# A transformer layer in split fp32: a new order at the front (opening of the row tiles, first convolution block among the query tiles, taps dealt from there)

## The chip, the core and the metric

The kernel runs on one core of a Trainium2 chip. TensorE multiplies matrices into PSUM, VectorE, ScalarE and GpSimd work on elements, and SyncE (SP) issues most transfers between HBM and SBUF. The metric is the device time of one execution in microseconds. The kernel before takes 1634.73 us (median of three runs, 1633.79 to 1635.66).

## The reference

One layer over 1024 rows of width 1024, all in float32. The parts that the change touches are the normalised rows, the memory branch's queries and the convolution; the rest stands as one line each.

```python
xn = rms_norm(x, norm_mix)
proj = xn @ w_in          # NSA queries, keys, values, gates; conv_in; q_mem; g_merge

# branch A: br_nsa, sparse attention (compressed, selected and windowed keys), 8 heads

# branch B: convolution
a, ag = jnp.split(conv_in, 2, axis=-1)
u = a * jax.nn.sigmoid(ag)
u = causal_depthwise_conv(u, conv_w, width=31) + conv_b
u = jax.nn.silu(layer_norm(u, conv_ln_g, conv_ln_b))
br_conv = u @ w_conv_out

# branch C: attention into 256 memory rows
qm = rms_norm(q_mem.reshape(b, s, 4, 128), mem_qk_norm[0])
kvm = rms_norm(mem, norm_mem) @ w_mem_kv
# ... softmax(qm km) vm, then br_mem = o_m @ w_mem_out

gm = jax.nn.sigmoid(g_merge).reshape(b, s, 3, 1024)
h = x + (gm[:, :, 0] * br_nsa + gm[:, :, 1] * br_conv + gm[:, :, 2] * br_mem) @ w_out
hn = rms_norm(h, norm_ffn)
return h + (silu(hn @ w_gate) * (hn @ w_up)) @ w_down
```

## The kernel before

**Arithmetic.** Every operand of a large product is split into a high part (a cast to `fp32r`, L131) and a low part (the value less its high part, L132). One product of the reference is three products on TensorE (high by high, low by high, high by low), gathered in one PSUM bank; `mm` (L146) emits them and lists them in `products`. A *unit* is a piece of a weight matrix of 128 partitions by 1024 elements with both its parts: ScalarE makes the high part, VectorE or GpSimd the low part.

**Rows.** The 1024 rows of x are eight row tiles of 128 rows, taken in four pairs. `norm_row` squares a row tile on ScalarE, takes the root there, and scales the tile on VectorE (L218). `turn_pair` then turns a pair by 16 TensorE transposes of 128x128 (L238) into four banks; ScalarE writes the high parts with the gain (L228, listed in `his`) and VectorE the low parts (L230, listed in `los`), eight instructions each. The rows so turned are `XN`, the operand of every projection.

**Memory queries.** `queries(ws, t, 0, rqm)` projects row tile t on the 512 query columns: 24 products of 128x512 (`wide_proj`, four weight units), then a copy on ScalarE (L345), a store to HBM by SP (L348), the square on ScalarE (L349) and its sum by heads on VectorE (L350). The loop runs over all eight tiles, and the second, third and fourth pair are turned behind tiles 1, 2 and 4. `square_queries` fetches the stored queries later and normalises and turns them (`t<-qraw`, `qt_m<-t`).

**Convolution.** Behind the queries come 35 small rows (31 taps of the filter, bias, two layer norm vectors: L444 to L448), which four transposes turn into `cw` (L451). Then four convolution blocks of 128 channels: two units, and for each half of the rows 24 products for the sigmoid's operand (`pg`), the sigmoid on ScalarE, 24 products for `pa`, and their product into `U`. Two `square_queries` follow each block. `weight_sums` (in the first block) loads pieces of `w_out`, makes differences of them on VectorE (`sub`, L128) and stores them as `tw`.

**Taps.** The filter itself is 124 VectorE instructions (31 for each of 4 blocks, `tap`, L485 and L486) of about 1000 columns. They are emitted at the end with a low priority and *dealt*: each is ordered behind a product of the list `products`, evenly by work, from `first_tap` (the count of products when the first convolution block is done) to the end of the projections. The turned keys (L745) come in the later part of that list.

**Filler.** The products of the merge gates (banks `pf`) have a low priority as well; TensorE takes them where nothing else is ready.

**What sets the order.** All instructions are emitted by one program in Python. A scheduler then orders each engine's queue by priority (mostly the order of emission) and by a model of the times; each engine runs its queue strictly in that order. `follow` and `add_manual_dep` add an order between two instructions without a wait on data. Banks, slabs and stages come from rotating pools.

Of the kernel before, what the change touches and what calls it, by code (L numbers as in the profile page):

```python
# [17 lines left out]
P = 128  # L18
# [21 lines left out]
def hybrid_layer_kernel(  # L40
# [127 lines left out]
    nc.vector.memset(ones, 1.0 / 512)  # L168
    strip = const([768], BF16, "strip")
# [40 lines left out]
    his, los = [], []  # L210
# [22 lines left out]
    def turned_pair(js, kp, after=None, at=None):  # L233
        b = bank([2, 256], at=at)
        for kk in range(2):
            k = 2 * kp + kk
            for tt in range(2):
                m = nc.tensor.transpose(b[:, kk, tt * P:(tt + 1) * P], js[tt][:, k * P:(k + 1) * P], ident)  # L238
                if after is not None:
                    follow(m, after, "tiles by turns with products")  # L240
        return b

# [5 lines left out]

    def rows2(src, r0):
        xs = slab([2, D], F32)  # L250
        for tt in range(2):
            nc.sync.dma_start(xs[:, tt, :], src[r0 + tt * P:r0 + (tt + 1) * P, :])
# [6 lines left out]
    def turn_x(tp):  # L259
        half, q = tp // 2, tp % 2  # L260
        if q == 0:
            for kp in range(4):
                XN[half][kp] = slab([2, 2, 512])
        turn_pair(xin[tp], 0, lambda kp: tuple(XN[half][kp][:, hl, :, q * 256:(q + 1) * 256] for hl in range(2)),
                  products[-12 if tp == 1 else -1][0] if tp else None)


    def unit(src, shape, alloc=wslab, eng=None, load=False, after=None):
# [8 lines left out]
        if after is not None:  # L277
            follow(m, after, "weights' cast behind attention's")
# [3 lines left out]
    def col_unit(w, c0, n=P, alloc=wslab, eng=None, load=False):  # L282
        return unit(w[:, c0:c0 + n].rearrange("(k p) c -> p k c", p=P), [w.shape[0] // P, n], alloc, eng,
                    load)
# [38 lines left out]

    def wide_proj(ws, t):

        o = bank([512])
        half, a = t // 4, (t % 4) * P
        if t == 0 and len(products) == 0:
            for k0 in (0, 4):
                for hx, hw in ((0, 0), (1, 0), (0, 1)):  # L330
                    for k in range(k0, k0 + 4):
                        mm(o, xn(hx, k, half, a, a + P), ws[k // 2][hw][:, k % 2, :], k + hx + hw == 0,
                           k == KT - 1 and hw == 1)
# [6 lines left out]
    def queries(ws, t, j, stat):  # L340
# [5 lines left out]
        if j == 0:  # L346
# [67 lines left out]
    ws = [wide_unit(w_in, C_QM, u, alloc=slab, eng=e) for u, e in enumerate((nc.vector, nc.gpsimd))]  # L414
    raw_w = [t4([2, 512]) for _ in range(2)]
    for u in range(2):
        nc.sync.dma_start(raw_w[u], wide_rows(w_in, C_QM, 2 + u))
    xin += [rows2(x, tp * 256) for tp in range(1, 4)]
    nc.sync.dma_start(gm, mem_qk_norm.to_broadcast([P, 2, P]))
# [4 lines left out]
    for raw, eng in zip(raw_w, (nc.gpsimd, nc.vector)):  # L424
        w_ = slab([2, 2, 512])
        m = nc.vector.tensor_copy(w_[:, 0], raw)
        follow(m, los[3], "behind the first tiles' parts")
        part = eng.tensor_tensor(w_[:, 1], raw, w_[:, 0].bitcast(F32), op=OP.subtract)
        if eng is nc.vector:
# [1242 lines left out]
```

## Time and profile before

| | us |
|---|---|
| median of three runs | 1634.73 |
| profiled execution | 1634.0 |
| its span (first to last instruction) | 1632.3 |
| TensorE busy | 1616.9 (99%) |
| TensorE's weight loads (beside its products) | 1361.7 (83%) |
| VectorE busy | 1097.7 (67%) |
| ScalarE busy | 759.1 (47%) |
| GpSimd busy | 662.3 (41%) |
| HBM read / written | 193.52 MB / 85.98 MB |

In the rows of the profile an engine is named PE (TensorE), PEld (TensorE's weight load), DVE (VectorE), ACT (ScalarE), POOL (GpSimd) or SP; a small q behind it is its sequencer. L345 is line 345 of the kernel. A row of the groups gives an operation, what it writes and reads, how often it runs, its busy time with the mean in ns, and the idle time of its engine ahead of it with what ended it. A row of the chain of waits gives when a step begins, how long it lasts, and in brackets how long it waited and for what. A row of the windows gives a stretch of time, its length, and then for each engine (PE, PEld, DVE, ACT, POOL) its busy time in that stretch with the number of its instructions, then the granted clock, the share of time in which the transfer engines were busy, and GB/s. A row of the transfers gives size and median time from issue to landing.

In the chain of waits, TensorE holds 92% of the span. The first products come at 10.8 us; before that lie loads, one row tile's scaling and its transposes.

### The profile page before, as it was taken

What the parts mean: (1) busy time and instruction counts of PE and PEld (TensorE: products, weight loads), DVE (VectorE), ACT (ScalarE), POOL (GpSimd) and SP (SyncE); (2) the same over time, 40 slices, a digit from 0 to 9 for tenths busy, and PEclk for the clock granted to TensorE, in tenths of its full rate; (3) what the DMA queues carried; (4) which work ended last, traced back from release to release, by engine and by line L of the source; (5) the groups of instructions that cost most, each with busy time, mean ns of one, the idle gap of its engine ahead of it and who ended that gap; (6) DMA issues with size and microseconds to landing.
All of it is one profiled execution on the core that took longest, in us unless ns stands there. A gap on an engine that the chain in (4) does not pass through costs nothing.

```text
span 1632.3 us, 22769 instructions
## 1 busy us (share of the span) xinstructions
PE 1616.9 (99%) x7952; PEld 1361.7 (83%) x7952; DVE 1097.7 (67%) x1821; ACT 759.1 (47%) x1404; POOL 662.3 (41%) x535
## 2 busy tenths in 40 slices
PE   8999999999999999999999999999999999999999
PEld 6887898888888888888888889888888888888887
DVE  6389989996676655654795968865455544476665
ACT  6211357634777756664684447332223222233332
POOL 2011003741777766654135341665556777300000
PEclk9999999999999999999999999999999999999999
DMA  8454457753555545546754453333234446893773
GB/s 293 170 170 118 134 163 202 240 166 109 154 172 174 172 138 152 164 143 231 241 179 157 165 194 136 97 113 114 90 112 147 142 152 199 314 383 101 238 232 117
DMA packets 254874, 281.03 MB, mean 172 GB/s; under 512 B 24404, under 2 KB 176260, under 8 KB 253222
## 3 DMA queue, kind: packets, MB, share of 16 engines
q1 hardware_dynamic: 247846, 266.98, 51.3%
q10 hardware_dynamic: 6912, 12.59, 2.1%
q8 instruction: 63, 1.03, 0.3%
q14 instruction: 53, 0.43, 0.1%
HBM read 193.52 MB, written 85.98 MB: 171 GB/s over the span
## 4 chain that ended last, share of the span: by engine, by line
PE 92%; DVE 3%; POOL 2%; issue 1%; DMA 1%; ACT 1%; SPq 0%; DVEq 0%; POOLq 0%; ACTq 0%
PE ps L146 52%; PE pf L146 19%; PE ps L1606 11%; PE ps L1374 4%; PE ps L1006 2%; PE pf L1606 1%; DVE slab L486 1%; PE ps L238 1%; PE pf L1374 1%; POOL slab L684 0%; PE ps L986 0%; DMA t<-qt_m 0%; DMA qt_n<-t 0%; POOL t L367 0%; DMA slab<-in_x_dram 0%
## 5 line engine op out<-in xcount | busy, mean ns | idle before, releaser
L146 PE MATMUL ps<-slab,wsl 128*128 128x512 f32 (+2 forms) x1688 | 362.5, 373 | 0.0
L146 PEld LDWEIGHTS ps<-slab,wsl 128*128 128x128 f32 x1688 | 298.3, 188 | 56.3 <-issue 1.0
L146 PE MATMUL pf<-slab,fsl 128*128 128x512 f32 x1260 | 320.9, 395 | 0.4 <-ACT fz L1081 0.4
L146 PEld LDWEIGHTS pf<-slab,fsl 128*128 128x128 f32 x1260 | 231.1, 188 | 44.0 <-ACT fz L1081 0.7
L486 DVE SCALAR_TENSOR_TENSOR slab<-slab,cw 128x1019 f32<-128x1019 f32 (+16 forms) x120 | 161.7, 1352 | 1.4
L1502 DVE TENSOR_TENSOR t<-ps,t 128x512 f32<-128x512 f32 x130 | 88.7, 687 | 105.8 <-PE ps L146 104.4
L146 PE MATMUL ps<-slab,fsl 128*128 128x512 f32 x660 | 155.9, 391 | 0.0
L146 PE MATMUL ps<-slab,slab 128*128 128x512 f32 (+1 forms) x628 | 150.9, 377 | 0.8 <-POOL slab L684 0.8
L146 PEld LDWEIGHTS ps<-slab,fsl 128*128 128x128 f32 x660 | 123.1, 188 | 25.5 <-issue 0.3
L146 PEld LDWEIGHTS ps<-slab,slab 128*128 128x128 f32 x628 | 112.5, 189 | 22.6 <-POOL slab L684 1.7
L1606 PE MATMUL ps<-wsl 128*128 128x512 f32 x495 | 118.9, 389 | 0.0
L1606 PEld LDWEIGHTS ps<-wsl 128*128 128x128 f32 x495 | 93.0, 188 | 19.2
L132 DVE TENSOR_TENSOR wsl<-st,wsl 128x1024 fp32r<-128x1024 f32 x58 | 82.6, 1428 | 29.3 <-ACT wsl L131 26.9
L146 PE MATMUL ps<-slab,qt 128*128 128x384 f32 (+6 forms) x400 | 95.6, 339 | 1.6 <-DVE sm L869 1.3
L131 ACT CAST wsl<-st 128x1024 fp32r<-128x1024 f32 x61 | 63.9, 1053 | 70.3 <-PE ps L146 25.0
L146 PE MATMUL ps<-wsl,slab 128*128 128x512 f32 (+1 forms) x480 | 95.3, 349 | 0.0
L131 ACT CAST wsl<-t 128x1024 fp32r<-128x1024 f32 x43 | 45.3, 1053 | 88.3 <-POOL t L128 35.4
L146 PE MATMUL ps<-t,slab 128*128 128x256 f32 (+1 forms) x404 | 86.2, 317 | 0.0
L132 POOL TENSOR_TENSOR slab<-slab,t 128x1024 fp32r<-128x1024 f32 (+1 forms) x28 | 63.0, 2250 | 55.8 <-ACT t L131 50.7
L146 PEld LDWEIGHTS ps<-wsl,slab 128*128 128x128 f32 x480 | 76.8, 189 | 10.4
L132 DVE TENSOR_TENSOR t<-ps,t 128x512 fp32r<-128x512 f32 (+2 forms) x96 | 61.0, 640 | 33.5 <-ACT t L131 32.7
L1515 POOL TENSOR_TENSOR t<-t,t 128x512 f32<-128x512 f32 x21 | 39.3, 1871 | 108.1 <-DVE t L1502 54.7
(270 smaller groups left out, 2950.9 us busy)
## 6 DMA issues: line engine op xcount, KB each, us to landing
t<-in_w_down_dram SPq DMA_DIRECT2D x70, 256.0 KB, 3.7
fst<-in_w_in_dram SPq DMA_DIRECT2D x24, 512.0 KB, 4.2
zd<-fz ACTq DMA_DIRECT2D x48, 256.0 KB, 2.0
slab<-wd SPq DMA_DIRECT2D x24, 512.0 KB, 4.0
t<-zd SPq DMA_DIRECT2D x24, 512.0 KB, 3.6
st<-in_w_gate_dram SPq DMA_DIRECT2D x22, 512.0 KB, 3.8
st<-in_w_up_dram SPq DMA_DIRECT2D x22, 512.0 KB, 4.1
ad<-t SPq DMA_DIRECT2D x44, 256.0 KB, 3.0
```

The source lines that it names most:

```text
L131: m = nc.scalar.copy(hi, src)
L132: return m, (eng or nc.vector).tensor_tensor(lo, src, hi.bitcast(F32), op=OP.subtract)
L146: m = nc.tensor.matmul(o, a, b, start=start, stop=stop)
L238: m = nc.tensor.transpose(b[:, kk, tt * P:(tt + 1) * P], js[tt][:, k * P:(k + 1) * P], ident)
L486: return nc.vector.scalar_tensor_tensor(acc[:, s:], u[:, :S - s], cw[:, ct, 30 - s:31 - s], acc[:, s:], op0=OP.mult, op1=OP.add)
L1006: nc.tensor.transpose(b[:, j - j0, h, :], tiles[h][:, j * P:(j + 1) * P], ident)
L1374: nc.tensor.matmul(B[j], a_(ha, k, j), w[:, hb, k % 2, :], start=start and k == 0 and n_ == 0, stop=stop and k == 3 and n_ == 2, skip_grou ...
L1502: nc.vector.tensor_tensor(o, a_, b_, op=OP.add)
L1515: nc.gpsimd.tensor_tensor(u4, u4, c22, op=OP.mult)
L1606: nc.tensor.matmul(B[t], a_, b_, start=start and k == 0 and j == 0, stop=k == FH - 1 and j == 2, skip_group_check=True)
```

## The change

It does six things, all within the program's first 100 us but for the taps.

1. **Constant products.** 26 bf16 products of a constant tile (`spin`, 128x256), whose result nobody reads, stand at the front of TensorE's queue.
2. **Opening.** `first_pair` turns the eight blocks of row tile 0 first, then those of row tile 1, into four banks. The four query units' raw values are all loaded ahead; the high parts of units 0 and 1 are made on VectorE, those of 2 and 3 on ScalarE behind the first pair's last high part; the low part of unit 2 on GpSimd, the others on VectorE, in a written order. Tiles 0 and 1 are multiplied by turns (`first_two`), and their last four products stand behind the second pair's transposes. Their copies stand behind that pair's high parts.
3. **Loads.** Three small loads (`gm`, `gn`, `w2s`) stand behind the row loads; the second pair's rows ahead of the gates' first weights, the third pair's rows behind them.
4. **First convolution block.** It runs behind the fourth query tile instead of the eighth, and the fourth pair of row tiles is turned inside it, between `pg` and `pa` of the first half. The small rows of the convolution and `weight_sums` move with it. Query tiles 4 to 7 follow.
5. **Taps.** `first_tap` is set behind that block, so that the 124 taps are dealt over a list that begins earlier.
6. **`square_queries`.** Three, three and two behind the blocks 1, 2 and 3, instead of two behind each of four.

The products of the layer are the same ones, in the same number.

```diff
+    spin = ones.bitcast(BF16)
+    b = psp[0].tile([P, 256], F32, tag="ps0", name=nm("ps"))
+    for _ in range(26):
+        nc.tensor.matmul(b, spin[:, :P], spin, start=True, stop=True)
...
     def turn_pair(src, g0, dests, after=None):
+        js = [src[:, tt, :] for tt in range(2)]
+        first = None if his else first_pair(js)
         for kp in range(4):
-            b = turned_pair([src[:, tt, :] for tt in range(2)], kp, after)
+            b = first[kp] if first else turned_pair(js, kp, after)
...
+    def first_pair(js):
+        banks, last = [bank([2, 256]) for _ in range(4)], None
+        for tt in range(2):
+            for k in range(KT):
+                m = nc.tensor.transpose(banks[k // 2][:, k % 2, tt * P:(tt + 1) * P], js[tt][:, k * P:(k + 1) * P], ident)
...
-        if t == 0 and len(products) == 0:
+        if not products:
+            first_two.append(bank([512]))
             for k0 in (0, 4):
-                for hx, hw in ((0, 0), (1, 0), (0, 1)):
+                for hx, hw, k1, k2 in ((0, 0, 0, 2), (1, 0, 0, 2), (0, 0, 2, 4), (1, 0, 2, 4), (0, 1, 0, 4)):
+                    for b, c in zip((o, first_two[0]), (0, P)):
...
-    ws = [wide_unit(w_in, C_QM, u, alloc=slab, eng=e) for u, e in enumerate((nc.vector, nc.gpsimd))]
-    raw_w = [t4([2, 512]) for _ in range(2)]
+    raw_w = [stage.tile([P, 2, 512], F32, tag="st", name=nm("st")) for _ in range(2)] + [t4([2, 512]) for _ in range(2)]
...
-    for raw, eng in zip(raw_w, (nc.gpsimd, nc.vector)):
+    for u in range(4):
         w_ = slab([2, 2, 512])
-        m = nc.vector.tensor_copy(w_[:, 0], raw)
-        follow(m, los[3], "behind the first tiles' parts")
+        high = (nc.vector.tensor_copy if u < 2 else nc.scalar.copy)(w_[:, 0], raw_w[u])
+        eng = nc.gpsimd if u == 2 else nc.vector
+        part = eng.tensor_tensor(w_[:, 1], raw_w[u], w_[:, 0].bitcast(F32), op=OP.subtract)
+        if u == 1:
+            tc.add_manual_dep(los[0], high.ins.name, ORDER, reason="low parts behind the first weights' high parts")
+        elif u > 1:
+            follow(high, his[7], "high part behind the first tiles'")
+        if u != 2:
+            follow(part, parts[-1] if u == 1 else los[7 if u else 3], "low part behind the first tiles'")
+    for m in los[4:8:2]:
+        tc.add_manual_dep(m, parts[1].name, ORDER, reason="low parts behind the first weights'")
...
-    for t in range(NT):
+    def memory_queries(t):
         queries(ws, t, 0, rqm)
-        if t in (1, 2, 4):
+        if t in (1, 2):
             turn_x((t + 2) // 2)
+            if t == 1:
+                tc.add_manual_dep(products[44][0], turns[-1].name, ORDER, reason="last products behind the second pair")
+                for m in copies:
+                    tc.add_manual_dep(m, his[-1].name, ORDER, reason="queries' copies behind the second pair")
+            rows_x(t // 2 + 2)
+    for t in range(4):
+        memory_queries(t)
...
-    for ct in range(4):
+    def conv_block(ct, between=None):
         for half in range(2):
             pg = chan_proj(wag, half)
+            if half == 0 and between is not None:
+                between()
...
+    conv_block(0, lambda: turn_x(3))
+    for t in range(4, NT):
+        memory_queries(t)
+    stat_rms(rqm)
+    for ct in range(1, 4):
+        conv_block(ct)
...
-        for t in (2 * ct, 2 * ct + 1):
+        for t in range(3 * ct - 3, min(3 * ct, NT)):
             square_queries(0, t, rqm)
```

How it stands in the engines' queues: a row is an instruction with its line, what it writes and reads (numbers tell buffers of one kind apart) and the semaphores that it waits for. First VectorE at the start, of before: `slab_142` holds the first pair of row tiles, `slab_153` unit 0, `st_151` its raw values, `slab_233` and `slab_236` units 2 and 3, `ps_...` turned blocks.

```order
L218 TENSOR_SCALAR slab_142<-slab_142,sm_190 128x1024 [waits DMAHW1_49,DVE_49]
L132 TENSOR_TENSOR slab_153<-st_151,slab_153 128x1024 [waits DMAHW4_49,Activation_49]
L230 SCALAR_TENSOR_TENSOR slab_193<-ps_197,gcol,slab_193 128x256 [waits PE_49,Activation_49]
...
L426 CAST slab_233<-t_10_161 128x1024 [waits DMAHW6_49]
L426 CAST slab_236<-t_11_162 128x1024 [waits DMAHW7_49]
L443 TENSOR_TENSOR spent<-spent 128x192 [waits DMAHW1_49]
L230 SCALAR_TENSOR_TENSOR slab_195<-ps_215,gcol,slab_195 128x256 [waits PE_49,Activation_49]
```

The same place of the change: `slab_254` and `slab_257` are units 0 and 1, `st_178` and `st_179` their raw values.

```order
L222 TENSOR_SCALAR slab_169<-slab_169,sm_211 128x1024 [waits DMAHW1_49,DVE_49]
L455 CAST slab_254<-st_178 128x1024 [waits DMAHW4_49]
L455 CAST slab_257<-st_179 128x1024 [waits DMAHW5_49]
L236 SCALAR_TENSOR_TENSOR slab_214<-ps_218,gcol,slab_214 128x256 [waits PE_49,Activation_49]
...
L457 TENSOR_TENSOR slab_254<-st_178,slab_254 128x1024 [waits DVE_49]
L457 TENSOR_TENSOR slab_257<-st_179,slab_257 128x1024 [waits DVE_49]
L236 SCALAR_TENSOR_TENSOR slab_216<-ps_220,gcol,slab_216 128x256 [waits PE_49,Activation_49]
```

The high parts of units 0 and 1 stand ahead of the tiles' low parts now, those of units 2 and 3 have left VectorE, and unit 1's low part stands behind unit 0's.

Second, SP's queue around the convolution's small rows, of the change (`t_82_516` holds the small rows, `t_80_508` is the copy of the fourth query tile, `t_91_546` to `t_94_549` are pieces of `w_out`). Before, it was the store of the eighth query tile that stood among these loads.

```order
L514 DMA t_94_549<-in_w_out_dram 128x2x512 [waits DMAHW0_49]
L520 DMA tw<-t_91_546 128x1024 [waits DMAHW1_49,DVE_49]
L487 DMA t_82_516<-in_conv_w_dram 31x512 [waits DMAHW2_49]
L376 DMA qraw<-t_80_508 128x512 [waits DMAHW3_49,Activation_49]
L488 DMA t_82_516<-in_conv_b_dram 1x512 [waits DMAHW4_49]
L489 DMA t_82_516<-in_conv_ln_g_dram 1x512 [waits DMAHW5_49]
L490 DMA t_82_516<-in_conv_ln_b_dram 1x512 [waits DMAHW6_49]
L496 DMA t_84_527<-in_cmp_pos_dram 16x2x128 [waits DMAHW7_49]
```

The three single rows and the position rows stand behind the store of the fourth query tile, which waits for ScalarE.

Third, TensorE's queue at the fourth pair of row tiles (`slab_171` before, `slab_192` in the change). Before:

```order
L146 MATMUL ps_487<-slab_236,slab_403 128x512 [waits DVE_49]
L238 MATMUL ps_518<-identr,slab_171 128x128 [waits DVE_49]
L238 MATMUL ps_527<-identr,slab_171 128x128 [waits PE_49]
...
L146 MATMUL ps_554<-slab_153,slab_400 128x512 x2
L238 MATMUL ps_518<-identr,slab_171 128x128 [waits DVE_49]
```

And in the change (`ps_578` is `pg` of the first half, `t_82_516` the convolution's small rows):

```order
L146 MATMUL ps_578<-slab_217,wsl_537 128x512 x6
L244 MATMUL ps_603<-identr,slab_192 128x128 [waits DVE_49,PE_49]
L244 MATMUL ps_630<-identr,slab_192 128x128 [waits Activation_49]
L493 MATMUL ps_521<-identr,t_82_516 128x34 [waits DMAHW5_49,DMAHW6_49,DMAHW4_49,DMAHW2_49]
L493 MATMUL ps_521<-identr,t_82_516 128x34 x3
L244 MATMUL ps_612<-identr,slab_192 128x128 [waits PE_49]
L244 MATMUL ps_603<-identr,slab_192 128x128 [waits DVE_49]
```

The four transposes of the small rows, with their wait for four loads, stand behind two of the fourth pair's blocks and ahead of the other fourteen; before, they stood among the products of the convolution.

More of the change, by code (lines that the diff above doesn't have):

```diff
@@ L240, in turned_pair @@
                     follow(m, after, "tiles by turns with products")
+        turns.append(m.ins)
         return b
+    def first_pair(js):
[3 more added lines that the diff above has]
+                m = nc.tensor.transpose(banks[k // 2][:, k % 2, tt * P:(tt + 1) * P], js[tt][:, k * P:(k + 1) * P], ident)
+                if last is not None:
+                    follow(m, last, "first row's blocks in front")
+                last = m.ins
+        return banks
     XN = [[None] * 4 for _ in range(2)]
@@ L247, in xn @@
         return XN[half][k // 2][:, hl, k % 2, a:b]
+    row_loads = []
     def rows2(src, r0):
@@ L277, in unit, with col_unit @@
         if after is not None:
-            follow(m, after, "weights' cast behind attention's")
+            follow(m, after, "weights' cast behind other work")
         casts.append(m.ins)
         return (w, ld.ins) if load else w
-    def col_unit(w, c0, n=P, alloc=wslab, eng=None, load=False):
+    def col_unit(w, c0, n=P, alloc=wslab, eng=None, load=False, after=None):
         return unit(w[:, c0:c0 + n].rearrange("(k p) c -> p k c", p=P), [w.shape[0] // P, n], alloc, eng,
-                    load)
+                    load, after)
     def row_units(w, c0, alloc=wslab, eng=None):
@@ L345, in queries @@
         m = nc.scalar.copy(raw, ps)
-        if j == 0:
+        copies.append(m.ins)
+        if j == 0 and t > 1:
             follow(m, roots[-1], "behind the next rows' roots")
@@ L423, in hybrid_layer_kernel @@
     turn_x(0)
[L424 removed]
+    ws = []
+    parts = []
+    for u in range(4):
         w_ = slab([2, 2, 512])
[L426 to L431 removed]
+        high = (nc.vector.tensor_copy if u < 2 else nc.scalar.copy)(w_[:, 0], raw_w[u])
+        eng = nc.gpsimd if u == 2 else nc.vector
+        part = eng.tensor_tensor(w_[:, 1], raw_w[u], w_[:, 0].bitcast(F32), op=OP.subtract)
+        ws.append((w_[:, 0], w_[:, 1]))
+        if u == 1:
[4 more added lines that the diff above has]
+            follow(part, parts[-1] if u == 1 else los[7 if u else 3], "low part behind the first tiles'")
+            parts.append(part.ins)
@@ L444, in hybrid_layer_kernel @@
+    for t in range(4):
+        memory_queries(t)
+    follow(nc.sync.dma_start(gn, nsa_qk_norm.to_broadcast([P, 4, 64])), row_loads[5].ins, "behind the rows")
+    follow(nc.vector.tensor_tensor(gn[:, 1:4, :], gn[:, 1:4, :], gn[:, 0, None, :].to_broadcast([P, 3, 64]), op=OP.mult),
+           los[15], "behind the second pair's low parts")
     rows = t2([512], p=TAPS + 3)
@@ L1069, in hybrid_layer_kernel @@
                 ws[n_] = col_unit(w_in, C_GM + b_ * D + d_ * P, alloc=fslab,
-                                  eng=nc.vector if n_ < N_EARLY else nc.gpsimd)
+                                  eng=nc.vector if n_ < N_EARLY else nc.gpsimd, load=n_ == 0,
+                                  after=None if n_ else roots[3])
+                if n_ == 0:
+                    ws[0], ld = ws[0]
+                    tc.add_manual_dep(ld, row_loads[1].ins.name, ORDER, reason="behind the second pair")
+                    for m in row_loads[2:4]:
+                        tc.add_manual_dep(m.ins, ld.name, ORDER, reason="third pair behind the gates' weights")
             w = ws[n_]
```

37 lines of the change are left out of this document (18 added, 19 removed).

## The prediction

> **What bounds the kernel now.** I read the page's busy line first, then a table of windows, then TensorE's waits.
>
> ```profile
> PE 1616.9 (99%) x7952; PEld 1361.7 (83%) x7952; DVE 1097.7 (67%) x1821; ACT 759.1 (47%) x1404; POOL 662.3 (41%) x535
> 0.00:20.00 20.00, 13.40 (x56) 10.96 (x57) 12.79 (x24) 12.78 (x25) 9.36 (x17) 1.00 0.94 329
> 20.00:60.00 40.00, 40.00 (x201) 33.40 (x200) 22.81 (x45) 24.49 (x53) 0.00 (x0) 1.00 0.49 155
> 60.00:100.00 40.00, 40.00 (x181) 32.90 (x180) 20.06 (x22) 7.47 (x11) 2.08 (x2) 1.00 0.79 267
> 100.00:240.00 140.00, 140.00 (x765) 118.93 (x764) 132.27 (x134) 43.30 (x82) 11.34 (x10) 1.00 0.45 136
> 240.00:400.00 160.00, 156.90 (x825) 133.65 (x824) 146.88 (x219) 86.86 (x212) 65.63 (x41) 1.00 0.61 183
> 400.00:560.00 160.00, 158.03 (x858) 135.00 (x857) 108.47 (x397) 117.65 (x330) 111.30 (x137) 1.00 0.54 160
> PE ps L745 <- DVE t L132: 1.6, 1, 1.6
> ```
>
> In the windows, the second number is the length, the third TensorE's busy time. TensorE is the bound: it idles 6.6 us of the first 20, nothing from 20 to 240, 3.1 us from 240 to 400 and 2.0 us from 400 to 560. So an edit gains only in the first 20 us or by shortening those 5.1 us; between 20 and 240 every wait it brings is paid in full. VectorE, at 92% from 240 to 400 (146.88 of 160), owns the largest wait, 1.6 us at the turned keys.
>
> The start, in order of time:
>
> ```profile
> 6.69 1.12 PE L238 MATMUL ps<-identr,slab 128*128 128x128 f32 x4 [0.55 <-DVE slab L218]
> 7.15 0.75 DVE L218 TENSOR_SCALAR slab<-slab,sm 128x1024 f32<-128x1024 f32 x1
> 7.92 1.05 ACT L131 CAST slab<-st 128x1024 fp32r<-128x1024 f32 x1 [1.00 <-DMA st<-in_w_in_dram]
> 7.96 2.82 PE L238 MATMUL ps<-identr,slab 128*128 128x128 f32 x12 [0.16 <-DVE slab L218]
> 9.00 1.22 DVE L132 TENSOR_TENSOR slab<-st,slab 128x1024 fp32r<-128x1024 f32 x1 [1.10 <-ACT slab L131]
> 9.27 1.05 ACT L131 CAST slab<-st 128x1024 fp32r<-128x1024 f32 x1 [0.30 <-DMA st<-in_w_in_dram]
> 10.22 3.02 ACT L228 ACTIVATE slab<-ps,gcol 128x256 fp32r<-128x256 f32 x8
> 10.39 2.38 POOL L132 TENSOR_TENSOR slab<-st,slab 128x1024 fp32r<-128x1024 f32 x1 [6.64 <-ACT slab L131]
> 10.79 11.64 PE ps L146 x48
> 11.08 1.66 DVE L230 SCALAR_TENSOR_TENSOR slab<-ps,gcol,slab 128x256 fp32r<-128x256 f32 x4 [0.86 <-ACT slab L228]
> 12.66 1.55 DVE L426 CAST slab<-t 128x1024 fp32r<-128x1024 f32 x2
> 22.27 1.91 PE L238 MATMUL ps<-identr,slab 128*128 128x128 f32 x16
> 35.19 0.60 PE L238 MATMUL ps<-identr,slab 128*128 128x128 f32 x4
> 50.53 9.55 PE ps L146 x42
> ```
>
> The two rows without an operand are of the chain of waits. A 128x512 product takes 9.55/42 = 0.227 us; a block turned takes 0.21 at first (12 in 2.82, less the tail) and 0.11 later (16 in 1.91): TensorE starts at half pace. Its first product waits until ScalarE, which first casts two weight units (7.92 and 9.27, each held up by its load), makes the first high parts at 10.22. For comparison with the changed start I take the stretch behind the second pair's blocks (22.27): 48 products (third query tile and a gate's) end at 35.19, so in effect that stretch begins at 35.19 - 48 x 0.227 = 24.3.
>
> **The change: the start.** Units 0 to 3 are the four 256-row pieces of the query weights. The 26 constant products can begin once `ones` is set, at about 1.1. A 256-column product is half of 0.227, 0.11, at full pace and 0.23 at half; so they end between 4.0 and 7.1, beside TensorE's idle time to 6.69. The late end would hold the gain column's copy, and row 1's scaling with it, about 0.5 us; unit 1's load, below, covers that. The second row is scaled at 7.15 + 0.75 = 7.9, its first turned bank stands by about 8.4 at full pace, and ScalarE's eight high parts run from 8.4 to 11.4 (3.02). The first product moves from 10.79 to about 8.8.
>
> What follows is VectorE's line. It now casts units 0 and 1; unit 1 lands only at 9.27 (ScalarE waited for it until then). Cast 0.78 (1.55/2): 10.05. Four low parts of the tiles, 1.66: 11.7. Unit 0's low part 1.22: 12.9. Then unit 1's low part. Meanwhile ScalarE casts unit 2 from 11.4 (1.05) and GpSimd's low part of it is ready to run at 12.5, so the two engines meet:
>
> ```profile
> 14.69 2.41 POOL L428 TENSOR_TENSOR slab<-t,slab 128x1024 fp32r<-128x1024 f32 x1
> 16.07 2.11 DVE L428 TENSOR_TENSOR slab<-t,slab 128x1024 fp32r<-128x1024 f32 x1
> ```
>
> Here the VectorE subtraction took 2.11 instead of 1.22, and ended 1.08 after GpSimd's (17.10 to 18.18): it waited for it. The Trainium skill, "SBUF — State Buffer", section "SBUF: two separate sides", calls the pair of ports that both use an exclusive lock held for a whole instruction; the rows agree, and by that rule GpSimd, queued at 12.5, would go next.
>
> If GpSimd goes first: 12.9 + 2.4 = 15.3, unit 1's low part at 15.3 + 1.08 = 16.4. TensorE stands there with 18 of its products done and 26 ahead of the second pair's blocks: 16.4 + 26 x 0.227 = 22.3, 16 blocks 1.75, the last 4 products 0.9: the third tile begins at 24.95 against 24.3, a **loss of 0.65**. If VectorE goes first: 14.1, and the third tile begins at 22.65, a **gain of 1.65**. GpSimd is ready 0.4 us ahead of VectorE's end, so I take the loss, +0.6. The second pair's scaling, now with its rows loaded ahead of the gate's weights, is ready before either.
>
> **The change: the fourth pair of row tiles (rows 6 and 7) between the two products of a convolution half.** Call P the start of the third pair's last 12 blocks (37.95 before). Products, ports and loads keep their distances to it:
>
> ```profile
> 37.95 1.47 PE L238 MATMUL ps<-identr,slab 128*128 128x128 f32 x12
> 38.47 3.02 ACT L228 ACTIVATE slab<-ps,gcol 128x256 fp32r<-128x256 f32 x8 [2.43 <-PE ps L238]
> 43.95 0.57 ACT L345 COPY t<-ps 128x512 f32<-128x512 f32 x1
> 44.42 0.60 ACT L349 ACTIVATE t<-ps 128x512 f32<-128x512 f32 x1
> 35.76 0.68 DVE L350 TENSOR_REDUCE rqm<-t 128x4 f32<-128x512 f32 x1
> 67.62 1.23 DVE L128 TENSOR_TENSOR t<-t,t 128x1024 f32<-128x1024 f32 x1 [5.01 <-DMA t<-in_w_out_dram]
> 66.85 0.35 SPq L348 DMA_DIRECT2D qraw<-t  x1
> 67.25 0.28 SPq L447 DMA_DIRECT2D t<-in_conv_ln_g_dram  x1
> 67.58 0.25 SPq L448 DMA_DIRECT2D t<-in_conv_ln_b_dram  x1
> L451 PEldq EVENT_SEMAPHORE  x2: 51/482/913, 72.5 to 72.7; - x2
> qt_m<-t SPq DMA_DIRECT2D x32, 64.0 KB, 2.0
> ```
>
> From P, TensorE does 12 blocks (1.3), 5 products and the sigmoid half's 24 (6.6), two of the fourth pair's blocks (0.2) and stands at P + 8.1 before the turned convolution rows. These need four small loads, three of which SP issues behind the store of the fourth query tile. ScalarE copies that tile behind eight high parts and two rows' squares: copy over at 44.52 - 37.95 = P + 6.57. SP: store 0.35, then loads spaced 0.33; the last of the rows, the bias of the layer norm, is issued at about P + 7.65. The quickest small transfer here (64 KB) lands 2.0 us after issue; the same row of before, behind full queues, was issued at 67.58 and TensorE's queue was released at 72.7 + 0.9 = 73.6, 6.0 later. So TensorE waits until P + 9.65 at least, P + 13.65 at most: **1.5 to 5.5 us**. A second chain ends alike: the copied tile's square is over at P + 7.07, its sum 0.68, one weight difference 1.23 and row 7's scaling 0.75 on VectorE, P + 9.75; the remaining blocks wait for it (1.6). Load queues are emptier there than in 68 to 76, so I stay near the low end: 2.0. Behind these blocks on TensorE stands everything else, and no other work is ordered ahead. The Trainium skill, "DMA: Bandwidth & Descriptors", section on the fixed cost, gives about 2.0 us per transfer; the wait by it would be 1.5.
>
> **The change: taps.** The 124 taps keep their cost and begin some 30 us earlier; in VectorE's order 115 of them, not 111, now stand ahead of the keys' first copy, and 80, not 73, ahead of the first softmax maximum.
>
> ```profile
> L486 DVE SCALAR_TENSOR_TENSOR slab<-slab,cw 128x1019 f32<-128x1019 f32 (+16 forms) x120 | 161.7, 1352 | 1.4
> ```
>
> Four taps of 1.35 are 5.4 us less on VectorE before the keys, more than the 1.6 us that TensorE waits: I take -1.6. At the other end a new wait of that size appears elsewhere in the same crowded stretch, +1.6. The earlier sums of the output weights, two more table loads on ScalarE and the moved stores cost nothing as long as TensorE's 24-product groups (5.4 us) cover them.
>
> **Sum.** +0.6 + 2.0 - 1.6 = +1.0 us: 1634.0 becomes 1635.0 (span 1632.3 and 1.7 around it). The median of the runs is 0.73 above the profiled execution: 1634.73 + 1.0 = **1635.7**. Its own bounds: -1.65 + 1.5 - 1.6 = -1.75 and 0.65 + 5.5 + 1.6 = +7.75.
>
> **Rivals.** *Faster:* VectorE's relief takes away all 5.1 us of TensorE's idle time from 240 to 560 and VectorE wins the port at the start: -1.65 + 1.5 - 5.1 = -5.25, 1629.5. For it: VectorE's 92%. Against it: after 400 the idle 2.0 us fall in attention, where no tap runs. *Slower:* the small rows take the 6.0 us of before, +0.6 + 5.5 - 1.6 = +4.5, 1639.2; it decides the sign once the last row lands over 4.8 us after issue. For it: the only landing that the trace shows for them. *The constant products don't raise the pace:* blocks of 0.21 make the first bank late by 0.9 us and ScalarE's unit 2 too, so VectorE gets the port first; with 0.7 for slow first products (11.64 against 48 x 0.227) the start gains 0.95 instead of losing 0.6: 1634.1.
>
> **Chances.** This kernel's measurement tells 0.2% (3.3 us) from no change. Forecast 0.55, pace not raised 0.05, both within: 0.60. Slower 0.21, faster 0.19. The range for 8 in 10 runs from 1631.0 to 1640.0, short of the faster rival's centre and past the slower one's.
>
> **What would show it.** Right: first product near 8.8; VectorE's second unit's low part about twice 1.22 long; TensorE idle some 2 us at the turned convolution rows near 49, released by a load or row 7's scaling; no 1.6 at the keys. Wrong: a low part of 1.22 and the third tile before 23.5; no wait near 49; new waits in attention beyond 2 us.

## The result and the profile after

The changed kernel takes 1645.78 us (median of six runs, 1644.12 to 1646.00) against 1634.77 us of the kernel before (six runs): 1.0065 of its time, 95% interval 1.0052 to 1.0078. It is 11.0 us **slower**, where 1.0 us (no change) was forecast, and lies outside the range of 1631.0 to 1640.0. The profiled execution took 1644.58 us, its span is 1642.8, 10.5 more than before.

The busy line and the windows of the changed kernel, in the same stretches as in the prediction (length, then TensorE, its weight loads, VectorE, ScalarE, GpSimd, granted clock, transfer share, GB/s):

```profile
PE 1624.4 (99%) x7978; PEld 1364.3 (83%) x7978; DVE 1096.0 (67%) x1822; ACT 760.8 (46%) x1406; POOL 651.7 (40%) x534
0.00:20.00 20.00, 18.74 (x90) 14.05 (x91) 13.83 (x26) 12.52 (x25) 6.33 (x14) 1.00 0.94 349
20.00:60.00 40.00, 33.10 (x163) 27.51 (x162) 25.08 (x47) 24.22 (x51) 1.00 (x2) 0.91 0.85 275
60.00:100.00 40.00, 40.00 (x179) 33.10 (x178) 31.15 (x31) 8.46 (x13) 0.00 (x0) 1.00 0.37 128
100.00:240.00 140.00, 140.00 (x760) 118.76 (x759) 119.21 (x123) 42.34 (x78) 13.16 (x10) 1.00 0.41 125
240.00:400.00 160.00, 155.05 (x819) 131.52 (x818) 144.86 (x212) 86.48 (x213) 60.63 (x42) 1.00 0.64 187
400.00:560.00 160.00, 158.63 (x847) 134.05 (x846) 99.60 (x376) 112.40 (x312) 102.97 (x134) 1.00 0.53 158
```

TensorE now idles 6.9 us between 20 and 60, where it idled not at all, and its clock there is 0.91. Its waits, longest first:

```profile
PE ps L493 <- DMA t<-in_conv_ln_b_dram: 5.3, 1, 5.3
PE ps L146 <- POOL slab L736: 2.1, 3, 1.5
PE ps L244 <- DVE sm L140: 1.6, 1, 1.6
PE ps L797 <- DVE t L132: 1.2, 2, 1.0
PE ps L146 <- DVE wsl L132: 1.0, 1, 1.0
```

L493 turns the convolution's small rows (L451 before), L244 turns row tiles, L797 turns the keys (L745 before). The chain of waits from 34 to 58 us tells how the first came about (start, length, what):

```profile
35.61 0.69 SPq L514
...
36.35 7.99 DMA t<-in_w_out_dram
...
44.43 1.23 DVE t L128
45.66 0.08 DVE sm L140
45.74 0.28 SPq L520
...
47.67 5.69 DMA t<-in_conv_ln_b_dram
53.36 0.14 issue
53.50 0.61 PE ps L493 x4
54.10 2.33 PE ps L244 x10
```

A piece of `w_out`, loaded for the weight differences, lands after 8.0 us. VectorE stands before the difference (L128) until then, and row 6, which has to be scaled behind it, comes 1.6 us late for TensorE. SP stands before the store of that difference (L520) until 45.7 with the small rows queued behind it (34 of them: 31 taps, the bias and two layer norm vectors); the last of these is issued at 47.67 and lands 5.7 us later. Then the ten blocks behind it take 2.33 us, 0.23 each instead of 0.11. TensorE's last blocks before that wait, in its timeline:

```profile
47.75 0.41 PE L244 MATMUL ps<-identr,slab 128*128 128x128 f32 x2 [1.56 <-DVE sm L140]
```

and the granted clock (the eighth figure of a window):

```profile
50.40:50.80 0.40, 0.00 (x0) 0.00 (x0) 0.40 (x1) 0.00 (x0) 0.00 (x0) 1.00 1.02 420
50.80:51.20 0.40, 0.00 (x0) 0.00 (x0) 0.39 (x1) 0.00 (x0) 0.00 (x0) 0.95 0.99 404
51.20:51.60 0.40, 0.00 (x0) 0.00 (x0) 0.00 (x0) 0.00 (x0) 0.00 (x0) 0.50 1.07 435
57.60:57.80 0.20, 0.20 (x2) 0.20 (x2) 0.20 (x2) 0.00 (x0) 0.00 (x0) 0.50 0.92 358
57.80:58.00 0.20, 0.20 (x1) 0.13 (x1) 0.20 (x1) 0.17 (x1) 0.00 (x0) 0.54 0.84 287
58.00:58.20 0.20, 0.20 (x2) 0.19 (x1) 0.20 (x2) 0.20 (x1) 0.00 (x0) 1.00 0.86 287
```

TensorE stopped at 48.2; 3 us later, near 51.2, its clock fell to half, and it came back near 58.0, 4.5 us after the restart at 53.5.

**Where the time went.** To place gains and losses along the program, each product of a trace is given the median pitch of its kind in the kernel before (from one start to the next). Added up in queue order this is the work done; a product's start less the work done is TensorE's lag; constant products count as no work. This is the lag of each kernel less that of the kernel before, in us, at given amounts of work (which is about the time less 10). The figures are good to some 0.3 us. Each row is one profiled execution, and that can lie up to 3 us off the median of its runs: the profiled one was the fastest of all for `after_frozen`, `after_frozen_busy` and `rows_in_time_frozen` (1.8, 3.0 and 1.9 below the median), the slowest for `start_frozen` and `start_frozen_no_constants` (1.1 and 0.7 above).

```
work done                      24    60   140   220   300   380   460   580   700   820  1580
changed kernel               -2.2  +7.2  +7.0  +6.9  +6.6  +9.6  +9.0  +9.9  +9.9  +9.9 +10.2
start_only                   -2.0  -1.9  -1.9  -1.6  +1.6  -0.6  -0.5  +0.4  +0.4  +6.1  +6.1
rows_early                   +5.0  +4.9  +4.7  +4.6  +4.6  +7.6  +6.9  +7.8  +7.8  +7.8  +7.8
sums_late                    -2.2  -1.3  -1.5  +7.4  +8.9  +7.8  +5.9  +7.9  +8.8 +11.1 +11.1
taps_late                    +0.8  +8.9  +8.7  +8.5  +9.6  +9.4  +9.0  +9.9  +9.9  +9.9  +9.9
constants_only               -0.6  -0.6  -0.6  -0.6  -0.5  +0.1  +0.5  +0.5  +0.5  +0.5  +0.5
start_frozen                 -1.8  -1.7  -1.7  -1.7  -1.7  -0.4  -0.1  -0.1  -0.1  +0.1  +0.1
start_frozen_no_constants    -0.8   0.0   0.0  +0.2  +0.2  -0.1  -0.1  -0.1  -0.1  -0.1  -0.2
after_frozen                 -2.4  +6.4  +6.2  +6.2  +6.2  +6.9  +6.8  +6.8  +6.8  +6.8  +6.8
after_frozen_busy            -2.0  +3.6  +3.4  +3.3  +3.4  +2.7  +2.9  +2.9  +2.9  +2.9  +2.9
sums_frozen                  -2.2  -1.1  -1.3  +0.1   0.0  +0.3  +0.2  +0.2  +0.2  +0.2  +0.2
start_frozen_no_gpsimd       -1.6  -1.6  -1.6  -1.5  -1.5  -1.4  -1.1  -1.1  -1.1  -1.1  -1.1
rows_in_time_frozen          -1.9  +0.3  +0.1  +0.1  +0.1  +0.8  +0.9  +0.9  +0.9  +0.9  +0.9
```

The changed kernel is 2.2 us ahead after the opening, loses 9.4 at the fourth pair of row tiles (TensorE's two waits of 1.6 and 5.3, the rest mostly half clock), and another 2.7 up to 580 (0.3 won before 220 and 3.0 lost behind it), where its code is that of the kernel before.

### The profile page after: what moved, and what is told of

Read it like the earlier page. It is cut to its first block, busy times and chain, and to the rows that moved or that the text cites. A ratio compares the mean times of both kernels' runs of the same rounds, so it can differ in the third digit from the quotient of the medians.

```text
span 1642.8 us, 22821 instructions
## 1 busy us (share of the span) xinstructions
PE 1624.4 (99%) x7978; PEld 1364.3 (83%) x7978; DVE 1096.0 (67%) x1822; ACT 760.8 (46%) x1406; POOL 651.7 (40%) x534
## 4 chain that ended last, share of the span: by engine, by line
PE 89%; DVE 5%; DMA 2%; ACT 1%; POOL 1%; issue 1%; SPq 1%; DVEq 0%; ACTq 0%; POOLq 0%
PE ps L146 50%; PE pf L146 18%; PE ps L1664 11%; PE ps L1432 4%; PE ps L1058 2%; PE pf L1664 1%; DVE slab L528 1%; PE ps L244 1%; PE pf L1432 1%; DVE wsl L132 0%; DMA t<-in_w_out_dram 0%; PE ps L1038 0%; PE ps L172 0%; DMA t<-in_conv_ln_b_dram 0%; DVE t L404 0%
## 5 line engine op out<-in xcount | busy, mean ns | idle before, releaser
L528 DVE SCALAR_TENSOR_TENSOR slab<-slab,cw 128x1023 f32<-128x1023 f32 (+14 forms) x120 | 163.7, 1364 | 1.5
```

What stands on the lines that cost most here:

```text
L528: return nc.vector.scalar_tensor_tensor(acc[:, s:], u[:, :S - s], cw[:, ct, 30 - s:31 - s], acc[:, s:], op0=OP.mult, op1=OP.add)
```

## The experiments

Each was timed beside the kernel before on the same chip; the ratios are against it.

**1. The opening alone.** `start_only` is the changed kernel with its convolution, taps and `square_queries` put back.

```diff
+        if t in (1, 2, 4):
+            turn_x((t + 2) // 2)
         if t in (1, 2):
-            turn_x((t + 2) // 2)
...
-    for t in range(4):
+    for t in range(NT):
         memory_queries(t)
+    stat_rms(rqm)
...
-    conv_block(0, lambda: turn_x(3))
-    for t in range(4, NT):
-        memory_queries(t)
-    stat_rms(rqm)
...
-    for ct in range(1, 4):
+    for ct in range(4):
         conv_block(ct)
...
-        for t in range(3 * ct - 3, min(3 * ct, NT)):
+        for t in (2 * ct, 2 * ct + 1):
             square_queries(0, t, rqm)
```

> The changed kernel with its opening and its moved loads alone (constants, first pair, weight units, first two tiles by turns, order of the loads); the convolution blocks, the taps and the square_queries stand as before. Theory A (the 2.2 us by which the changed kernel is ahead at the third query tile stay to the end): 2.2 us faster than before, 1632.6. Theory B (VectorE, 92% busy from 240 to 400, gives them back as new waits there): no change, 1634.8, with the 2.2 us of idle time in that stretch.

Measured: 1640.34 us, ratio 1.0039 (1.0027 to 1.0052). Both theories fall: an opening that is 2 us shorter made the kernel 6 us slower. The lag stays near -1.9 up to 140 and is -1.6 at 220; then 3.2 come and 2.1 go between 220 and 460, and 5.7 are lost near 785, where TensorE waits behind a late load of the convolution's sums. First the chain of waits, then TensorE's timeline and a window:

```profile
784.35 0.34 SPq L988
...
784.74 3.33 DMA slab<-ud
788.08 1.03 ACT wsl L131
789.11 1.00 ACT t L131 x2
790.11 0.50 ACT slab L1237
...
789.64 0.38 PE L146 MATMUL ps<-t,slab 128*128 128x256 f32 x1 [1.38 <-ACT t L131]
...
790.00:795.00 5.00, 4.38 (x14) 3.44 (x14) 4.17 (x4) 2.55 (x6) 1.65 (x1) 0.69 0.84 295
```

TensorE's stops there are short (0.3, 1.4 and 0.6 us), yet its clock falls to half behind them, from 791.9 to 795.3 (0.69 on average in the window). The same happens once more in this trace, from 303.8 to 307.2, behind two stops of 1.0 and 1.3 us.

No line of the code there was changed. But the order of the queues was: the scheduler plans with a model of the times, and with another opening it placed hundreds of products and VectorE instructions, and these loads, elsewhere from 200 us on.

**2. The small rows earlier.** `rows_early` emits the five loads, the small transposes and the two copies behind the second query tile.

```diff
     for t in range(4):
         memory_queries(t)
+        if t == 1:
+            conv_rows()
```

> The changed kernel with the convolution's small rows (five loads, six small transposes, two copies) moved to behind the second query tile. Theory A (of the 9.3 us lost at the fourth pair of row tiles, 5.3 are the wait for these rows, 1.6 and some more are row 6 and 7 scaled late because VectorE stands before a weight difference whose load is late, and 2.2 are the half clock that follows a long stop): the rows' wait and the half clock go, some 3.3 us stay for rows 6 and 7; 6 us faster than the changed kernel, 1639.8. Theory B (the place itself is bad: whatever TensorE finds there waits for the crowded load queues until about 53 us): no more than 1 us is won, 1645.

Measured: 1642.30 us, ratio 1.0047 (1.0032 to 1.0062). The wait moved along with the rows:

```profile
PE ps L488 <- DMA t<-in_conv_ln_b_dram: 3.8, 1, 3.8
```

TensorE now stands at 28 us until 32, loses 6.5 us with the half clock, and then nothing at the fourth pair. So the place, which B blames, is not at fault, but the rows land late in the new place too: they are queued behind two stores and among the big loads. In the time 3 us are won on the changed kernel, between A's 6 and B's 1. Beyond 100 us its queues stand in the changed kernel's order, and it loses as much there: from +4.6 at 220 to +7.8 at 580.

**3. The weight differences later.** `sums_late` moves `weight_sums` from the first block to the second.

```diff
-        if ct == 0:
+        if ct == 1:
             weight_sums()
```

> The changed kernel with the weight differences (loads of w_out, four differences, stores, twice) moved from the first convolution block to the second. Theory A (the store of the first difference waits on SP for VectorE, and VectorE for the load of w_out, 8.0 us; the small rows and row 6 stand behind them): the wait at row 6 goes, the small rows are issued some 2 us earlier into emptier queues; 2 to 3 us of the 9.3 stay, 1638.5. Theory B (the store of the fourth query tile's copy alone sets when the rows are issued, as the prediction had it, and they take 6 us to land): 6 to 7 us of wait and half clock stay, 1643.

Measured: 1643.77 us, ratio 1.0055 (1.0040 to 1.0070). At the fourth pair theory A holds, and better than it said: 0.9 us are lost instead of 9.4. SP's queue and TensorE's there:

```profile
44.54 0.36 SPq L376 DMA_DIRECT2D qraw<-t  x1
44.94 0.28 SPq L489 DMA_DIRECT2D t<-in_conv_ln_g_dram  x1
45.26 0.25 SPq L490 DMA_DIRECT2D t<-in_conv_ln_b_dram  x1
47.63 0.43 PE L493 MATMUL ps<-identr,t 34*128 34x34 f32 x4
```

Without the 2 MB of `w_out` in the queues the last row, issued at 45.26, is there for a product at 47.63. Between 140 and 220 us of work this kernel loses 8.9 us, in another order of its queues and with two more falls of the clock (at 160.7 and 218.8 us), and 3.7 more by the end. So its time is near B's 1643, though not for B's reason.

**4. The taps dealt as before.** `taps_late` sets `first_tap` behind the eighth query tile.

```diff
     stat_rms(rqm)
+    first_tap = len(products)
```

> The changed kernel with the taps dealt from the end of the eighth query tile, as before the change (first_tap behind query tile 7). Theory A (the earlier deal of the taps costs the 2.9 us that TensorE loses between 240 and 560): 2 to 3 us faster than the changed kernel, 1643. Theory B (those 2.9 us come from any new order of the queues, not from the deal): within 1 us of the changed kernel, or slower.

Measured: 1644.01 us, ratio 1.0057 (1.0042 to 1.0072), not to be told from the changed kernel's 1.0065. In the lag it loses 1.4 between 220 and 580 instead of 3.0, which leans to A, but the scheduler's order changed with the deal, so the two are not parted by this run. Its profile shows something else: it comes out of the opening 3.0 us behind the changed kernel with the same instructions in it. VectorE and GpSimd, first of the changed kernel:

```profile
9.10 0.69 DVE L455 CAST slab<-st 128x1024 fp32r<-128x1024 f32 x1 [0.39 <-DMA st<-in_w_in_dram]
11.28 2.35 DVE L457 TENSOR_TENSOR slab<-st,slab 128x1024 fp32r<-128x1024 f32 x2
13.55 1.65 DVE L236 SCALAR_TENSOR_TENSOR slab<-ps,gcol,slab 128x256 fp32r<-128x256 f32 x4
12.70 3.20 POOL L457 TENSOR_TENSOR slab<-t,slab 128x1024 fp32r<-128x1024 f32 x1 [8.93 <-ACT slab L455]
```

and of `taps_late`:

```profile
9.52 0.69 DVE L455 CAST slab<-st 128x1024 fp32r<-128x1024 f32 x1 [0.64 <-DMA st<-in_w_in_dram]
11.70 4.55 DVE L457 TENSOR_TENSOR slab<-st,slab 128x1024 fp32r<-128x1024 f32 x2
12.56 2.61 POOL L457 TENSOR_TENSOR slab<-t,slab 128x1024 fp32r<-128x1024 f32 x1 [8.80 <-ACT slab L455]
```

Unit 1 landed 0.4 us later. In the first trace VectorE was in its second subtraction when GpSimd came, and GpSimd took 3.20; in the second GpSimd came first, and the two VectorE subtractions took 4.55 instead of 2.35. Between these two traces 0.4 us in a load went with 3.0 us at the end of the opening. (The changed kernel's own runs lie in two groups, two at 1644.1 and 1644.6 and four at 1645.8 to 1646.0. Whether GpSimd came first in the upper group is not shown: only one run, of the lower group, has a trace.)

**5. The constants alone.** `constants_only` is the kernel before with the 26 products at the front; no other queue changes.

```diff
     nc.vector.memset(ones, 1.0 / 512)
+    spin = ones.bitcast(BF16)
+    b = psp[0].tile([P, 256], F32, tag="ps0", name=nm("ps"))
+    for _ in range(26):
+        nc.tensor.matmul(b, spin[:, :P], spin, start=True, stop=True)
```

> The kernel before with the 26 constant products at TensorE's front and nothing else; every other queue stands as before. Theory A (the constants raise TensorE's pace by 6.5 us, so that the 16 first blocks take 0.11 and the first products 0.227): 1.6 + 0.7 = 2.3 us faster than before, 1632.3. Theory B (they raise it, but the first product waits for ScalarE, which casts two weight units first, and so the faster blocks are not seen): the 0.7 us of the slow first products alone, 1633.9. Theory C (the pace doesn't depend on them): no change.

Measured: 1633.90 us, ratio 0.9997 (0.9988 to 1.0006). In the lag 0.6 us are won, as B says, and given back near 320 us; the time can't be told from that of the kernel before, so the runs don't part B from C.

**6 and 7. The order of the kernel before, kept.** To part the edit from the scheduler's answer to it, everything emitted from the gate keys on (11,203 instructions, the taps and the gates' products among them) is ordered on each engine as in the kernel before, by a table of numbers. `start_frozen` does this to `start_only`, `after_frozen` to the changed kernel.

```diff
+    emitted = nc.cur_f.blocks[-1].instructions
+    for steps in json.loads(zlib.decompress(base64.b85decode(TABLE))):
+        at, last = 11203, None
+        for d in steps:
+            at -= d
+            i_ = emitted[len(emitted) - 1 - at]
+            if last is not None:
+                tc.add_manual_dep(i_, last, ORDER, reason="order of the kernel before")
+            last = i_.name
```

> The kernel with the changed opening alone (start_only), and everything emitted from the first gate keys on ordered on each engine as in the kernel before, by a table; what is left of the difference stands in the first 30 us. Theory A (what start_only lost between 220 and 800 us, 8 us, comes from the scheduler's other order there): it keeps the opening's 1.9 us, 1632.5. Theory B (VectorE and the loads are as full there whatever the order, and an earlier arrival is given back): 1634.3 or more.

> The changed kernel, with everything emitted behind the last convolution block's square_queries ordered on each engine as in the kernel before (the taps too). Theory A (the 2.9 us lost between 220 and 580 come from the scheduler's new order): TensorE stays 7.0 us behind the kernel before from 100 us to the end, 1641.3. Theory B (they come from the earlier first block, or from the late arrival): 1644 to 1646 as the changed kernel.

Measured: `start_frozen` 1633.19 us, ratio 0.9990 (0.9981 to 0.9999), `after_frozen` 1643.09 us, 1.0048 (1.0036 to 1.0061). For `start_frozen` theory A holds in the main: with the old order `start_only`'s 1640.34 becomes 1633.19. B has a part in it: the trace shows 1.7 us kept up to 300 and 1.3 given back by 380; the runs say 1.2 kept. For `after_frozen` the trace is as A says, 6.4 us behind at 60 us of work and 6.8 at the end. But it is the fastest of five runs; their median is 1.8 above A's 1641.3, 8.7 above the kernel before where the changed kernel is 11.0 above, and the two intervals overlap. So for the changed kernel A is shown by the trace and not by the times.

**8. The opening without constants.** `start_frozen_no_constants` leaves the 26 products out of `start_frozen`.

```diff
-    for _ in range(26):
-        nc.tensor.matmul(b, spin[:, :P], spin, start=True, stop=True)
```

> start_frozen without the 26 constant products. Theory A (half pace until some 5 us of work are done): the 16 first blocks cost 1.7 us more and the first products 0.7, of which ScalarE's eight high parts hide some; 1.5 to 2.4 us slower than start_frozen. Theory B (VectorE's line sets when the products run through): under 0.5 us.

Measured: 1633.62 us, ratio 0.9994 (0.9985 to 1.0003). In the traces it is 1.7 behind `start_frozen` at 60 us of work, as A has it: there the whole gain of the opening comes through the constants. In the time only 0.4 are left of it, which is what B said and less than the intervals can tell. So the traces speak for A and the runs do not confirm it.

**9. TensorE kept at work in the wait.** `after_frozen_busy` puts 46 constant products between the first half's sigmoid products and the small rows' transposes. Nobody reads them; the layer's own work is all there.

```diff
-    b = bank([4, TAPS + 3])
+    b = bank([512])
+    held = [nc.tensor.matmul(b[:, :256], spin[:, :P], spin, start=True, stop=True) for _ in range(46)]
+    b = b[:, :4 * (TAPS + 3)].rearrange("p (a b) -> p a b", a=4)
...
     def between():
+        follow(held[0], products[-1][0], "constants behind the first half's products")
```

> after_frozen with 46 constant products (128x256, 0.107 us each at full pace, 4.9 us) on TensorE between the first half's sigmoid products and the small rows' transposes, that is inside the wait for the small rows. Theory A (of the 9.3 us lost there 2.2 are the half clock that follows TensorE's long stop): the wait still ends near 53.4, the blocks behind it run at 0.11 instead of 0.23, about 2 us faster than after_frozen, 1641.1. Theory B (the blocks behind are slow for another reason, crowded transfers): no gain, 1643.1 or more.

Measured: 1640.08 us (five runs, 1637.09 to 1642.15), ratio 1.0036 (1.0023 to 1.0048), 3.0 faster than `after_frozen` (five runs, 1641.26 to 1643.41); the intervals overlap, so the clock's part is read from the traces. TensorE's timeline:

```profile
45.73 5.20 PE L580 MATMUL ps<-ones 128*128 128x256 bf16 x46
51.26 0.41 PE L583 MATMUL ps<-identr,t 34*128 34x34 f32 x4 [0.34 <-DMA t<-in_conv_ln_b_dram]
51.60 0.29 PE L590 MATMUL ps<-identr,t 16*128 16x16 f32 x2
51.82 1.97 PE L332 MATMUL ps<-identr,slab 128*128 128x128 f32 x16
```

Sixteen blocks take 1.97; the clock stays at 1.00. Of the 3.1 us less that this trace loses here (5.6 against 8.7) 1.5 come from rows that happened to land earlier (51.2 against 52.7), and 1.6 to 1.7 from the clock. That is the half clock's price, somewhat under the 2.2 I had put down.

**10. The differences later, in the old order.** `sums_frozen` is `sums_late` with the table.

> sums_late (the weight differences in the second convolution block) with everything emitted behind the convolution blocks ordered as in the kernel before. Theory A (the late sums cost nothing by themselves; sums_late lost its 10 us behind 150 us by the scheduler's new order): the place of the fourth pair costs 0.9, the opening gains 2.2, 1633 to 1634. Theory B (the sums' loads and differences stand in the way of the weights and of VectorE wherever they are, as the 3.4 us wait at 157 us of sums_late suggests): 1637 to 1641.

Measured: 1634.71 us, ratio 1.0004 (0.9995 to 1.0013): 0.7 above theory A's range and 2.3 below B's. With the differences out of the way and the old order behind it, the kernel with the convolution block between the query tiles can't be told from the kernel before. The block is not free, though: the lag is -2.2 after the opening, -1.1 behind the fourth pair and +0.2 at the end, and `start_frozen`, which has the same opening and not the block, is 1.5 faster, at the edge of what the runs can tell.

**11. No GpSimd in the opening.** `start_frozen_no_gpsimd` gives the low part of unit 2 to VectorE.

```diff
-        eng = nc.gpsimd if u == 2 else nc.vector
+        eng = nc.vector
...
-        if u != 2:
+        if u < 4:
```

> start_frozen with the low part of unit 2 on VectorE instead of GpSimd (unit 2 and 3 behind the first pair's last low parts). Theory A (whichever of GpSimd and VectorE comes first at about 12.5 us holds the other up, and where GpSimd comes first the opening loses 2 us or more): without GpSimd no run has that, the median is within 0.5 us of start_frozen and its runs lie closer, 1633.0. Theory B (VectorE's line gets too long: the second pair's scaling ends 0.6 us later): 0.6 us slower than start_frozen, 1633.8.

Measured: 1632.93 us, ratio 0.9992 (0.9984 to 1.0001), eleven runs from 1632.15 to 1633.13 but for one of 1634.73. Median and, but for that one, spread are as A says. This and `start_frozen` are the fastest kernels of the study, 1.2 us under the kernel before, at the edge of what the runs can tell.

**12. The small rows ahead of the store.** `rows_in_time_frozen` is `after_frozen` with the five loads emitted behind the third query tile, so that on SP they stand behind the loads of `w_out` and ahead of the first difference's store. The transposes keep their place.

```diff
     for t in range(4):
         memory_queries(t)
+        if t != 2:
+            continue
+        crows = t2([512], p=TAPS + 3)
+        nc.sync.dma_start(crows[0:TAPS, :], conv_w[0, :, 0, :])
...
+        nc.sync.dma_start(prow, cmp_pos[0].rearrange("s (m a) d -> m s (a d)", a=2))
```

> after_frozen with the five loads of small rows emitted behind the third query tile, so that on SP they stand ahead of the first weight difference's store instead of behind it (still behind the loads of w_out); their transposes keep their place. Theory A (the store's wait for VectorE on SP is what made the rows late; VectorE's own stand before the difference still holds up rows 6 and 7): no wait at the small rows, two waits of about 1.5 us at row 6 and row 7, no half clock; 3 us of the 8.7 stay, 1635.2. Theory B (the rows are late because the load queues are full until 52 us): wait and half clock stay, 1643.

Measured: 1636.66 us, ratio 1.0020 (1.0011 to 1.0029), eleven runs from 1634.75 to 1639.64. Both theories have a part. The chain:

```profile
40.44 7.29 DMA t<-in_conv_ln_b_dram
47.74 0.14 issue
47.87 0.40 PE ps L585 x4
48.27 0.48 PE ps L332 x3
```

The last row is issued 7.2 us earlier than in the changed kernel, as A says, but takes 7.3 us to land behind the 2 MB of `w_out`, as B says; TensorE waits 1.9 once, the clock stays at 1.00, and rows 6 and 7 are scaled in time for their blocks. In this trace, of the fastest run, 2.2 us stay of the 8.7; in the medians the kernel is 2.8 above the kernel before, where `after_frozen` is 8.7 above.

## Why the prediction was wrong

**The opening: the wrong one of two branches, both well priced.** First product forecast at 8.8, measured 9.2. For GpSimd first I gave the third tile at 24.95, for VectorE first at 22.65. The traces, reckoned in the same way (48 products of 0.227 back from the third pair's first blocks, at 35.90 and 33.27), show 25.0 (`taps_late`) and 22.4 (the changed kernel). The choice rested on "GpSimd is ready 0.4 us ahead of VectorE's end", which counted from unit 1's landing at 9.27; it landed at 9.1 and 9.5 in these two traces. It is a race, and should have gone into the sum as a chance of each branch, not as the one term +0.6. A low part of 1.22 with the third tile before 23.5, which the changed kernel shows, was among the prediction's own signs of being wrong.

**The fourth pair: 2.0 forecast, 9.4 measured.** This is the step that failed: the wait of TensorE at the small rows was put at 2.0, near the low end of its 1.5 to 5.5. Three things were missed.

- *What the differences wait for.* I listed "one weight difference 1.23" on VectorE's chain and the store of the fourth query tile on SP. In the row I quoted for it stood that VectorE had been idle 5.01 us ahead of the difference, for a load of `w_out`. In the changed kernel that load takes 8.0 us and holds up two queues: VectorE, behind it row 6 (1.6 us), and through the difference's store SP, behind it the small rows (issued 2.0 later than my 45.7).
- *The landing.* "Load queues are emptier there than in 68 to 76, so I stay near the low end" was wrong: the change brings the 2 MB of `w_out` there too, and the transfer engines are busy 85% of 20 to 60 us. It landed in 5.7, not near the 2.0 of the quickest transfers; the 6.0 of the kernel before was the right price and stood in the bounds. With the `w_out` loads gone it was 2.4 at most (run 3).
- *The clock.* In the stop of 5.3 us TensorE fell to half clock; so it did in the 3.8 us of run 2. The change's own constants had this as their theme, and I priced a wait of up to 5.5 us without it. Run 9 puts it at 1.6 to 1.7 us. The Trainium skill, "TensorE: Matmul & The Clock Gate", part 1 ("The HAM clock gate"), says that the clock halves after an idle window of about 3.4 us and comes back after about as long at work. The changed kernel's trace agrees for the fall (3.0 us into the stop) and shows 4.5 for the return; but in `start_only` the clock fell with no stop over 1.4 us.

**The taps: -1.6 forecast, +2.7 to 3.0 in that stretch.** The keys' wait shrank from 1.6 to 1.2, and others grew (2.1 for GpSimd's L736, the line that cost 0.8 before, 1.0 for a weight's low part). All told TensorE idles 6.3 us between 220 and 580 us instead of 5.1; the rest of the loss is products that follow each other a little more slowly, and its cause was not found. Four taps fewer ahead of the keys was a true count, but not the change that mattered: runs 1 and 6 show that the scheduler's new order can cost this much on its own, with the taps dealt as before, and in run 7's trace, with the whole order held, the taps' too, 0.6 of the 3.0 are left. The prediction followed the order at the places of the edit and counted the taps; the rest of the queues it took to stand as before. How the 2.7 divide between the deal and the order stays open (run 4).

**The sum.** -2.2 + 9.4 + 2.7 + 0.3 (lost near 1030 us) = 10.2, the lag of the profiled execution; the median is 1.2 above that execution, where the forecast had 0.7.

**The rivals.** The slower one named the right mechanism, small rows that take 6 us to land, and came to 1639.2; it lacked the 8.0 us load ahead of them, the clock, and the order, and had the opening with the wrong sign. The constants did raise the pace: the blocks took 0.11.

## What to carry to other kernels

When loads are moved, ask what queue they stand in and what waits in that queue behind them: here loads of 2 MB held VectorE, VectorE held a store on SP, and the store held the 68 KB of small rows that TensorE needed. Add the price of the slow restart (1.6 us here) where TensorE may stop for a few microseconds, and also where short stops crowd together (`start_only`). And where a scheduler plans with a model of the times, an edit at the front is two edits: compare its order to the end of the program, and test the edit with the rest of the order held as it was; here that made 7 us of difference for the very same edit.

## What was new on the hardware

In these traces VectorE and GpSimd held up each other's 128x1024 subtractions until the one under way had ended, in both directions: on VectorE one of 1.22 us took 3.42 behind GpSimd (4.55 for two), on GpSimd one took 3.20 behind VectorE instead of 2.4 to 2.6. VectorE's low parts of row tiles, which read PSUM, were not held up: beside GpSimd's 3.20 four of them took the usual 1.65.

The granted clock changes, in all fourteen traces, only at the ends of stretches of 3.41 us counted from its first rise. From full clock it fell behind every stretch in which TensorE was idle for 1.8 us or more in all (3.0 at the fourth pair; 2.05 and 1.8 in `start_only`, in pieces of at most 1.4) and behind none with 1.7 or less. The stop of 1.9 us in `rows_in_time_frozen` lay across the end of a stretch, with 1.7 of it in the first, and cost no clock.

A 2 KB row took from under 2.4 us to 7.3 us to land, by what stood ahead of it. And with the same order of the queues, a lead won in the first 25 us was given back between 300 and 380 us in some traces (0.6 of `constants_only`, 1.3 of `start_frozen`) and kept in another (`start_frozen_no_gpsimd`, 0.1 lost); what sets the time at that point was not found.
